# Encoder block on one core: weight scales, neighbourhood bias and gate operands issued in another order

## The chip, the cores and the metric

The kernel runs on one core of a Trainium2 chip. The core has five engines, each of which works through its own queue of instructions in order: PE (TensorE, the matmuls), DVE (VectorE), ACT (ScalarE), POOL (GpSimd) and SP (SyncE, which here issues nearly all DMAs). They wait for one another by semaphores. The metric is device time in microseconds (us); smaller is better.

## The reference

One encoder block on `x` of 1 x 1024 x 1024 in float32: LayerNorm, one wide projection, two attentions beside each other, gates, an output projection and an MLP.

```python
h = layer_norm(x, ln0_g, ln0_b)
proj = h @ w_in + b_in                       # 1024 x 1024 times 1024 x 4352
qa, ka, va, qb, kb, vb, ga, gb = jnp.split(proj, IN_SPLITS, axis=-1)
...
y_na  = neighbourhood_attention(qa, ka, va, na_rpb) @ w_branch_na    # 8 heads, 16 x 64 grid, 8 x 16 window
y_swa = windowed_gqa_with_sink(qb, kb, vb, swa_sink) @ w_branch_swa  # 8 query heads, 2 key heads
mixed = jax.nn.sigmoid(ga) * y_na + jax.nn.sigmoid(gb) * y_swa
h = layer_norm(DEEPNORM_ALPHA * h + mixed @ w_out + b_out, ln1_g, ln1_b)
u = jnp.square(jax.nn.relu(h @ w_ff1 + b_ff1))
h = layer_norm(DEEPNORM_ALPHA * h + u @ w_ff2 + b_ff2, ln2_g, ln2_b)
```

In the neighbourhood attention each head adds a learned bias, `na_rpb`, to its scores before the softmax.

## The kernel before

**Arithmetic.** Every large product is made of 16-bit matmuls. A 32-bit operand is scaled by a power of two and split into a 16-bit `hi` and the 16-bit rest `lo`; `gemm3` and `gemm3_steps` (L399) add hi x hi, hi x lo and lo x hi. The normalised input `h` lies transposed in `hT[:, 0]` (hi) and `hT[:, 1]` (lo), in two halves of 512 tokens. What was 32 bits before the split, the tile `t` of `ln0_turn`, is overwritten later.

**Weight chunks.** `Chunk` holds 1024 x 128 columns of `w_in`, loaded by one DMA of 512 KB. Its method `to(n)` takes it through four states: 1, the squares are summed (ACT, L209); 2, the sum over the partitions (PE, a small f32 matmul, L194), the scale from it (DVE, L196) and its power of two (POOL, `pow`, L198); 3, `hi` (ACT, L236); 4, `lo` (DVE, L238). In attention, `blocks` runs 24 such chunks as fillers, 48 matmuls each. `ahead` puts the states of the next chunk off by so many filler matmuls: `D_C` = 4, 12, 18 for states 2, 3, 4, and 36 for state 1 of the chunk behind it (`D_C0` for the first).

**Stages**, by the times of the profiled execution. Up to 52 us (first stage): `x` comes in, LayerNorm, 64 transposes for each half of the tokens, `ln0_turn` (ACT makes `t`, L368; ACT or DVE makes `hi`; DVE or POOL makes `lo`), and between them the gates of the first two chunks `ws[0]` and `ws[1]`, four times 24 matmuls. A loop over `i` places all this; `LAG` and `LAG2` say how many `i` a gate lies behind the transposes that it reads, `HI_AT` at which `i` the `hi` of `ws[1]` is made, `PRE_AT` at which `i` the third chunk gets its states, and `warm(n)` issues `n` matmuls on zeros. From 52 to 97 us: projections. From 97 to 411 us: attention, one call of `steps(s)` for a quarter of a head: the scores of s + 2 (`part_a`, PE L729 and L730, DVE L731), the exponentials (`part_l`, `part_e`, ACT L750 and L753), the values of s - 1 (`part_c`, PE L837, then ACT L843 and DVE L846 take the result out of PSUM), and filler matmuls between these by `pump`. From 411 to 494 us: the gates' last columns (gate sums). They are computed by a scheme of Strassen's kind with seven products (`STEPS`) for each of four column pairs `p`; its operands are sums of quarters of `h` (A11, A12, A21, A22), formed on DVE by `f_add` (L1135) from the `hi` and `lo` of the quarters (`part`), and sums of quarters of the weights `graw` (`g_sums` L1064, `g_hi` L1080, `g_lo` L1084); `g_do` issues the matmuls (L1095), and `g_after` adds the results up (L1158). From 494 us on: branches, output projection and MLP.

**Order.** PE, ACT, DVE, POOL and SP are scheduled by hand (`manual_schedule`): each engine runs its instructions in the order in which the program issues them, and an instruction that waits holds up all behind it on its engine. `defer` puts a step behind a number of filler matmuls, `flush` issues those that are due.

**Two helpers of attention.** `na_bias(h)` loads a table `tb` and issues eight POOL operations at once: one scaling (L537) and seven adds that make the bias tile `bm` (L541). `proj_na_qk` allocates for the first two heads the tile `kl` and clears half of it on POOL at once (L505).

**Weights of the gate sums.** `g_load(p)` loads the pair `p` in iteration H = 12 + p of the loop over heads; `g_squares` sums its squares on ACT (L209) in H = 13 + p, `g_total` makes its scale after that.

Of the kernel before, what the change touches and what calls it, by code (L numbers as in the profile page):

```python
# [92 lines left out]
def encoder_block(ctx, tc, x, w_in, w_br, w_out, w_ff1, w_ff2, par, rows, rpbp,  # L93
# [96 lines left out]
    def scale_of(ps, sums_, exp=True):  # L190
        j = n_sc[0]
        n_sc[0] += 1
        for i, c in enumerate(sums_):
            PE.matmul(ps[:, 0:2], one0, c.to_broadcast([P, 2]), start=(i == 0), stop=(i == len(sums_) - 1))  # L194
# [1 line left out]
        DVE.scalar_tensor_tensor(out=t, in0=ps[:, 0:2], scalar=Q_MIN, in1=cv0, op0=ALU.max, op1=ALU.mult)  # L196
        if exp:
            POOL.tensor_tensor(out=wsc[:, 2 * j:2 * j + 2], in0=t, in1=pw0, op=ALU.pow)  # L198
# [7 lines left out]
    def square_sum(raw):  # L206
        i = n_sq[0] % 40
        n_sq[0] += 1
        ACT.activation(junk0, raw.rearrange("p k n -> p (k n)"), AF.Square, accum_out=wsq[:, i:i + 1], saturate=False)  # L209
# [11 lines left out]
    class Chunk:  # L221
# [6 lines left out]
        def to(self, n, ps=None, exp=True):  # L228
            while self.n < n:
# [3 lines left out]
                elif self.n == 2:  # L233
                    self.sc, self.back = scale_of(psum("t") if ps is None else ps, [self.sq], exp)
                elif self.n == 3:
                    ACT.activation(self.pair[:, 0], self.raw, AF.Copy, bias=0.0, scale=self.sc)  # L236
# [263 lines left out]
    def proj_na_qk(h, w, store):  # L500
        q = ap.tile([P, S], F32R, tag="q", name="q", bufs=3)
        kk = ap.tile([P, S], F32R, tag="kh", name="kh")
        if h < 2:
# [1 line left out]
            POOL.memset(b32(na_ql[h][64:P]), 0.0)  # L505
# [27 lines left out]

    def na_bias(h):
        tb = ap.tile([P, 16, 3, 8], F32, tag="x2", name="tb", bufs=1)
        nc.sync.dma_start(tb.rearrange("p a g c -> p (a g c)"), rpbp[h])
        POOL.tensor_scalar(out=tb, in0=tb, scalar1=8.0, scalar2=None, op0=ALU.mult)  # L537
        bm = ap.tile([P, 896], F32, tag="x1", name="bm")
        for o, g0, n, m in ((0, 0, 3, mk[:, 0:384]), (384, 1, 2, mk[:, 384:640]), (640, 0, 2, mk[:, 384:640])):
            for g in range(n):  # L540
                POOL.tensor_tensor(  # L541
                    out=bm[:, o + g * P:o + (g + 1) * P].rearrange("p (a c) -> p a c", c=8),
                    in0=tb[:, :, g0 + g, :],
                    in1=m[:, g * P:(g + 1) * P].rearrange("p (a c) -> p a c", c=8), op=ALU.add)
# [1842 lines left out]
```

## Time and profile before

| | us |
|---|---|
| time, median of 3 runs | 1276.07 |
| the runs | 1273.51 to 1277.71 |
| the profiled execution, its own time | 1273.13 |
| its span, first to last instruction | 1271.3 |
| PE busy | 1226.5 (96%) |
| DVE busy | 958.2 (75%) |
| ACT busy | 849.7 (67%) |
| POOL busy | 338.2 (27%) |

The page cuts the span into 40 slices of 31.8 us and gives the busy share of each in tenths; `PEclk` is the clock that the throttle granted to PE, in tenths of full speed, and `DMA` the mean busy share of the 16 DMA engines. For shorter stretches the trace is asked by windows (busy time, count and granted clock in a stretch), by waits (who waited for whom), by groups of equal instructions and by time (one row for an instruction, or for several alike, with its start, its length and, in brackets, the idle time before it and what ended that).

### The profile page before, as it was taken

To read this page: it belongs to the slowest core of one execution; us is meant where nothing else is said; L and a number is where in the kernel's file an instruction comes from. 1 tells how busy PE (TensorE), PEld (TensorE's weight loads), DVE (VectorE), ACT (ScalarE), POOL (GpSimd) and SP (SyncE) were. 2 spreads that over 40 slices of the span, in tenths; PEclk is the share of its full clock that TensorE was granted. 3 is DMA by queue.
4 is the path that set the end of the run, shared out by engine and by line. 5 is a ranking of instruction groups with operands and counts; after the bars stand their busy time and mean duration, and the time that the engine had idled before them with its cause. 6 is when DMAs were issued, how large, how long until landed. Compare 5 with 4: busy or idle time off the path is not lost.

```text
span 1271.3 us, 16827 instructions
## 1 busy us (share of the span) xinstructions
PE 1226.5 (96%) x6026; PEld 672.3 (53%) x6026; DVE 958.2 (75%) x1360; ACT 849.7 (67%) x1368; POOL 338.2 (27%) x353
## 2 busy tenths in 40 slices
PE   7999998899889989999999999999999999999997
PEld 4446555455445436888885444444444444444443
DVE  6678996677657986444687987787776678898888
ACT  6568887888888546442557877877877746435457
POOL 5362222242230000334741013233300001211207
PEclk8999999899999999999999999999999999999999
DMA  5345666457757224656342257676637635363333
GB/s 236 134 181 114 156 148 152 116 129 141 165 147 193 61 91 150 198 192 221 116 167 94 107 179 258 239 247 201 226 140 265 231 132 224 124 245 136 124 108 133
DMA packets 165780, 210.53 MB, mean 166 GB/s; under 512 B 110400, under 2 KB 112192, under 8 KB 159424
## 3 DMA queue, kind: packets, MB, share of 16 engines
q1 hardware_dynamic: 164720, 208.59, 51.8%
q8 instruction: 47, 0.77, 0.2%
q10 hardware_dynamic: 976, 0.87, 0.2%
q14 instruction: 37, 0.30, 0.1%
HBM read 127.55 MB, written 56.18 MB: 145 GB/s over the span
## 4 chain that ended last, share of the span: by engine, by line
PE 72%; ACT 10%; DVE 9%; DMA 4%; issue 2%; POOL 1%; SPq 1%; ACTq 0%; POOLq 0%; DVEq 0%
PE ps_mm L399 12%; PE ps_o L1620 6%; PE ps_t L1620 6%; PE ps_s L2092 6%; PE ps_mm L2092 6%; PE ps_mm L1620 5%; PE ps_t L2092 5%; PE ps_o L2092 4%; DMA pt<-pl 3%; PE ps_s L1620 2%; ACT ss L750 2%; PE ps_o L837 1%; ACT pl L753 1%; PE ps_t L390 1%; PE ps_t L389 1%
## 5 line engine op out<-in xcount | busy, mean ns | idle before, releaser
L399 PE MATMUL ps_mm<-hT 128*128 128x512 f16 x1248 | 298.1, 382 | 5.5 <-DVE hT L196 2.2
L1620 PEld LDWEIGHTS <-tw 128*128 128x128 f16 x1248 | 122.1, 99 | 145.0 <-issue 1.7
L399 PEld LDWEIGHTS <-hT 128*128 128x128 f16 x1248 | 117.8, 100 | 131.2 <-issue 17.3
L2092 PEld LDWEIGHTS <-hS 128*128 128x128 f16 x1008 | 98.6, 98 | 118.3
L750 ACT ACTIVATE ss<-ss,sk 128x384 f32<-128x384 f32 (+1 forms) x128 | 74.1, 580 | 28.5 <-DVE sk L731 27.9
L1620 PE MATMUL ps_t<-hS,tw 128*128 128x512 f16 x384 | 87.9, 379 | 0.0
L762 DVE SCALAR_TENSOR_TENSOR pl<-ss,pl 128x640 f16<-128x640 f32 (+1 forms) x64 | 72.1, 1127 | 1.3 <-ACT pl L753 0.9
L1810 DVE TENSOR_TENSOR usl<-usl 128x512 f32<-128x512 f32 x64 | 51.5, 804 | 23.5 <-ACT usl L1738 23.3
L1375 POOL TENSOR_TENSOR mx<-sg 128x512 f32<-128x512 f32 x16 | 32.5, 2032 | 133.6 <-DMA sg<-sg_d 82.7
L1541 POOL TENSOR_TENSOR c<-c 128x2 f32<-128x2 f32 x16 | 15.5, 974 | 193.5 <-DVE c L1540 193.5
L2112 POOL TENSOR_TENSOR acc<-acc,rst 128x512 f32<-128x512 f32 x16 | 31.3, 1958 | 123.0 <-DMA rst<-xr_d 100.7
L753 ACT ACTIVATE pl<-ss 128x640 f16<-128x640 f32 (+1 forms) x64 | 50.6, 790 | 11.6 <-DMA pt<-pl 9.8
L837 PE MATMUL ps_o<-pt,vv 128*128 128x256 f16 (+1 forms) x448 | 49.7, 251 | 8.5 <-DVE oT L846 8.1
L1095 PEld LDWEIGHTS <-hT 128*128 128x128 f16 x336 | 32.9, 99 | 46.5 <-DVE hT L1084 5.3
L238 DVE SCALAR_TENSOR_TENSOR hT<-hT 128x1024 f16<-128x1024 f32 x26 | 35.4, 1362 | 28.0 <-ACT hT L236 27.9
L1925 DVE SCALAR_TENSOR_TENSOR hS<-stg,c,hS 128x2048 f16<-128x2048 f32 x21 | 49.9, 2378 | 7.6 <-ACT hS L1922 7.6
L1547 DVE SCALAR_TENSOR_TENSOR tw<-raw,c,tw 128x512 f16<-128x512 f32 x60 | 51.8, 864 | 4.7 <-ACT tw L1544 4.3
L198 POOL TENSOR_TENSOR hT<-hT 128x2 f32<-128x2 f32 x29 | 23.6, 816 | 116.7 <-DVE hT L196 116.6
L2092 PEld LDWEIGHTS <-hA 128*128 128x128 f16 x336 | 32.9, 98 | 39.6
L837 PEld LDWEIGHTS <-vv 128*128 128x128 f16 x448 | 35.7, 98 | 26.2 <-DVE oT L846 10.1
L1620 PE MATMUL ps_o<-hS,tw 128*128 128x512 f16 x192 | 44.0, 379 | 0.0
L1544 ACT ACTIVATE tw<-raw,c 128x512 f16<-128x512 f32 x60 | 41.7, 708 | 2.8 <-DVE raw L1585 2.8
(395 smaller groups left out, 3006.3 us busy)
## 6 DMA issues: line engine op xcount, KB each, us to landing
us_d<-usl SPq DMA_DIRECT2D x112, 256.0 KB, 2.9
stg<-us_d SPq DMA_DIRECT2D x28, 1024.0 KB, 4.8
hT<-in_w_in SPq DMA_DIRECT2D x26, 512.0 KB, 4.5
raw<-in_w_ff SPq DMA_DIRECT2D x24, 512.0 KB, 5.5
sg<-sg_d SPq DMA_DIRECT2D x32, 256.0 KB, 3.4
hA<-in_w_ff SPq DMA_DIRECT2D x8, 1024.0 KB, 8.0
hS<-in_w_ff SPq DMA_DIRECT2D x8, 1024.0 KB, 7.6
sg_d<-hT SPq DMA_DIRECT2D x16, 256.0 KB, 3.1
```

Source lines behind the costliest of these rows:

```text
L238: DVE.scalar_tensor_tensor(out=self.pair[:, 1], in0=self.raw, scalar=self.sc, in1=self.pair[:, 0], op0=ALU.mult, op1=ALU.subtract)
L399: PE.matmul(ps, a[:, k, :], act(b, k), start=(k == 0 and i == 0), stop=(k == NK - 1 and i == 2))
L750: ACT.activation(p, p, AF.Exp, bias=nm[:, i:i + 1], scale=-1.0, accum_out=sums_l[o_chunk][:, hh, 2 * t + i:2 * t + i + 1])
L753: ACT.activation(pl[:, 0:n_all], e[:, 0:n_all], AF.Copy, bias=0.0, scale=P_SCALE)
L762: DVE.scalar_tensor_tensor(out=pl[:, n:2 * n], in0=e[:, 0:n], scalar=P_SCALE, in1=pl[:, 0:n], op0=ALU.mult, op1=ALU.subtract)
L837: PE.matmul(o, vs, move(part), start=(m == 0 and part == 0), stop=(m == len(runs) - 1 and part == 1))
L1544: ACT.activation(hi_lo(slot, 0), src, AF.Copy, bias=0.0, scale=w_scale(p))
L1547: DVE.scalar_tensor_tensor(out=hi_lo(slot, 1), in0=src, scalar=w_scale(p), in1=hi_lo(slot, 0), op0=ALU.mult, op1=ALU.subtract)
L1620: PE.matmul(ps, ww, act[:, part, k, :], start=(first and k == 0 and m == 0), stop=(k == 3 and m == 2), skip_group_check=True)
L1810: DVE.tensor_tensor(out=out, in0=a, in1=b, op=op)
L1925: DVE.scalar_tensor_tensor(out=slot[:, :, 1, :], in0=src, scalar=scale, in1=slot[:, :, 0, :], op0=ALU.mult, op1=ALU.subtract)
L2092: PE.matmul(ps, st[:, a, part, j * P:(j + 1) * P], w[:, a, wpart, :], start=(first and a == 0 and m == 0), stop=(a == 3 and m == 2), skip_ ...
```

## The change

Nothing that is computed changes, up to rounding in the quarter sums. Five things are ordered or made in another way:

1. `Chunk.to` has five states: the sum over the partitions (state 2, PE) is apart from the scale (state 3, DVE and `pow` on POOL); `hi` is state 4, `lo` state 5. In attention, within a block of 48 filler matmuls the next chunk's sum and scale come after 2 (4 before), its `hi` after 18 (12 before), its `lo` after 28 (18 before), and the squares of the chunk behind it after 32 (36 before).
2. First stage: the squares and the sum of `ws[1]` move into the first loop over `g`, its `hi` from i = 4 to i = 1, and the gate of `ws[1]` for the first half of the tokens follows that of `ws[0]` after one `i` (three before). `warm` at that place issues two matmuls in place of four.
3. The eight POOL operations of `na_bias` go into a list, from which each call of `steps` takes three; the clearing of `kl` moves behind the projection that fills the tile.
4. The squares of the gate sums' weights are made on DVE in place of ACT, and loads, squares and scales of these weights come one head earlier.
5. `ln0_turn` stores the 32-bit `t` of the quarters A11, A12 and A22 to DRAM (`hq_d`, 12 DMAs of 256 KB, issued by SP); the gate sums load them (3 DMAs of 1 MB, into `gq`, `gq2`, and `gq` again), so that three operand sums take one DVE operation each in place of two. The order of the calls in the gate sums changes with it.

```diff
-LAG2 = 3
+LAG2 = 1
-HI_AT = 4
-PRE_AT = {9: 1, 12: 2, 16: 3, 18: 4}
-D_C = 4, 12, 18, 36
-D_C0 = 16, 26, 32, 38
+HI_AT = 1
+PRE_AT = {9: 1, 12: 3, 16: 4, 18: 5}
+D_C = 2, 18, 28, 32
+D_C0 = 12, 22, 32, 40
-WARM = 18, 4, 4, 2, 0, 4
+WARM = 18, 4, 4, 2, 0, 2
+    hq_d = {q: dp.tile([P, 4, 512], F32, name=f"hq_d{q}") for q in ("A11", "A12", "A22")}
...
-    def scale_of(ps, sums_, exp=True):
+    def total_of(ps, sums_):
+        for i, c in enumerate(sums_):
+            PE.matmul(ps[:, 0:2], one0, c.to_broadcast([P, 2]), start=(i == 0), stop=(i == len(sums_) - 1))
+
+    def scale_of(ps):
...
+        if on_dve:
+            DVE.scalar_tensor_tensor(out=junk0, in0=flat, scalar=1.0, in1=flat, op0=ALU.mult, op1=ALU.mult,
+                                     accum_out=wsq[:, i:i + 1], saturate=False)
...
                 elif self.n == 2:
-                    self.sc, self.back = scale_of(psum("t") if ps is None else ps, [self.sq], exp)
+                    self.ps = psum("t") if ps is None else ps
+                    total_of(self.ps, [self.sq])
                 elif self.n == 3:
+                    self.sc, self.back = scale_of(self.ps)
+                elif self.n == 4:
...
+        q = f"A{half + 1}{k // 4 + 1}"
+        if q in hq_d:
+            nc.sync.dma_start(hq_d[q][:, k % 4], t)
...
-            POOL.memset(b32(na_ql[h][64:P]), 0.0)
...
             def lo(cs=cs, b=b):
+                if h < 2 and cs.start == 0:
+                    POOL.memset(b32(ql[64:P]), 0.0)
...
+        bias_ops.append(lambda: POOL.tensor_scalar(out=tb, in0=tb, scalar1=8.0, scalar2=None, op0=ALU.mult))
...
-                POOL.tensor_tensor(
+                bias_ops.append(lambda o=o, g0=g0, m=m, g=g: POOL.tensor_tensor(
...
+            if g == 3:
+                ws[0].to(3)
             ln0_stats(g)
             if g == 3:
-                ws[0].to(2, start_ps[:, 2:4], False)
+                ws[1].to(2, start_ps[:, 4:6])
...
+            if g == 2:
+                ws[0].to(2, start_ps[:, 2:4])
+                ws[1].to(1)
...
-            if i == 1:
-                ws[1].to(1)
-            if i == 3:
-                ws[1].to(2, start_ps[:, 4:6])
+            if i == 0:
+                ws[1].to(3)
...
             if before_b:
                 before_b()
+            for op in bias_ops[:3]:
+                bias_ops.pop(0)()
             flush(False, True)
...
-            gsq[p, c] = square_sum(graw[p][c])
+            gsq[p, c] = square_sum(graw[p][c], True)
...
+        gq2 = x0p.tile([P, 4, 512], F32, tag="m", name="gq2")
+        nc.sync.dma_start(gq, hq_d["A11"])
+        nc.sync.dma_start(gq2, hq_d["A12"])
...
-        f_add(g2, g1, part("A11", 0), ALU.subtract)
-        f_add(g2, g2, part("A11", 1), ALU.subtract)
+        f_add(g2, g1, gq, ALU.subtract)
+        nc.sync.dma_start(gq, hq_d["A22"])
-        f_add(g1, part("A12", 0), g2, ALU.subtract)
-        f_add(g1, g1, part("A12", 1))
+        f_add(g1, gq2, g2, ALU.subtract)
-        f_add(g2, part("A22", 0), g2, ALU.subtract)
-        f_add(g2, g2, part("A22", 1))
+        f_add(g2, gq, g2, ALU.subtract)
```

What this does to the queues is shown at three places, each with the rows of one engine in the order of the program (line, operation, tile written and tiles read, shape).

POOL in attention, where the first neighbourhood heads begin (at 211 to 220 us of the profile). The rows that write `hT` 128x2 are the `pow` of a weight chunk. Before:

```order
L198 TENSOR_TENSOR hT<-hT 128x2
L537 TENSOR_SCALAR tb<-tb 128x384
L541 TENSOR_TENSOR bm<-tb,mk 128x128 x7
L505 MEMSET kl 64x1024
L198 TENSOR_TENSOR hT<-hT 128x2
```

and of the changed kernel:

```order
L200 TENSOR_TENSOR hT<-hT 128x2
L534 MEMSET kl 64x1024
L551 TENSOR_SCALAR tb<-tb 128x384
L554 TENSOR_TENSOR bm<-tb,mk 128x128 x2
L200 TENSOR_TENSOR hT<-hT 128x2
L554 TENSOR_TENSOR bm<-tb,mk 128x128 x5
```

The second `pow` stood behind eight bias operations and the clearing of `kl`; now it stands behind three bias operations.

ACT in the first stage: `ln<-ln,mv` is the normalisation, L209 the squares, L236 a chunk's `hi`, L367 and L368 the evacuations of `ln0_turn`. Before:

```order
L341 ACTIVATE ln<-ln,mv 128x1024
L236 ACTIVATE hT<-hT 128x1024
L368 ACTIVATE t<-ps_t,hT 128x512
L368 ACTIVATE t<-ps_s,hT 128x512
L209 ACTIVATE hT<-hT 128x1024
L367 ACTIVATE hT<-ps_o,hT 128x512
```

and of the changed kernel, where these lines are 348, 243, 375, 213 and 374:

```order
L348 ACTIVATE ln<-ln,mv 128x1024
L213 ACTIVATE hT<-hT 128x1024
L243 ACTIVATE hT<-hT 128x1024
L375 ACTIVATE t<-ps_t,hT 128x512
L375 ACTIVATE t<-ps_s,hT 128x512
L243 ACTIVATE hT<-hT 128x1024
L374 ACTIVATE hT<-ps_o,hT 128x512
```

The squares of `ws[1]` moved ahead of the `hi` of `ws[0]`, and the `hi` of `ws[1]`, which stood seven instructions behind those squares, took their place.

DVE in the gate sums: the rows with 128x2048 are `f_add` (`g` and `gt` hold 32-bit sums, `gS` is the 16-bit `lo`). Before:

```order
L1135 TENSOR_TENSOR gS_4156<-g_3917,gS_4156 128x2048
L1084 SCALAR_TENSOR_TENSOR hT<-gT_4215,hT 128x512
L1135 TENSOR_TENSOR g_3917<-hT,gt 128x2048
L1084 SCALAR_TENSOR_TENSOR hT<-graw,hT 128x512
L1135 TENSOR_TENSOR g_3917<-g_3917,hT 128x2048
L1084 SCALAR_TENSOR_TENSOR hT<-graw,hT 128x512
L1158 SCALAR_TENSOR_TENSOR go<-ps_s,hT,go 128x512 x2
L1135 TENSOR_TENSOR gt<-hT,gt 128x2048
L1135 TENSOR_TENSOR gS_4158<-g_3917,gS_4158 128x2048
```

and of the changed kernel:

```order
L1154 TENSOR_TENSOR gS_4173<-g_3941,gS_4173 128x2048
L1180 SCALAR_TENSOR_TENSOR go<-ps_s,hT,go 128x512
L1104 SCALAR_TENSOR_TENSOR hT<-graw,hT 128x512
L1154 TENSOR_TENSOR g_3941<-gq_4177,gt 128x2048
L1104 SCALAR_TENSOR_TENSOR hT<-graw,hT 128x512
L1180 SCALAR_TENSOR_TENSOR go<-ps_s,hT,go 128x512
L1154 TENSOR_TENSOR gt<-gt 128x2048
L1154 TENSOR_TENSOR gS_4175<-g_3941,gS_4175 128x2048
```

Between the `lo` of one operand (first row) and that of the next (last row) stood three long sums; now there are two, and both read a loaded quarter where `hi` and `lo` were read before.

More of the change, by code (lines that the diff above doesn't have):

```diff
@@ L188, in encoder_block, with square_sum @@
     n_sc = [0]
-    def scale_of(ps, sums_, exp=True):
+    def total_of(ps, sums_):
+        for i, c in enumerate(sums_):
+            PE.matmul(ps[:, 0:2], one0, c.to_broadcast([P, 2]), start=(i == 0), stop=(i == len(sums_) - 1))
+    def scale_of(ps):
         j = n_sc[0]
         n_sc[0] += 1
-        for i, c in enumerate(sums_):
-            PE.matmul(ps[:, 0:2], one0, c.to_broadcast([P, 2]), start=(i == 0), stop=(i == len(sums_) - 1))
         t = wt[:, 2 * j:2 * j + 2]
         DVE.scalar_tensor_tensor(out=t, in0=ps[:, 0:2], scalar=Q_MIN, in1=cv0, op0=ALU.max, op1=ALU.mult)
-        if exp:
-            POOL.tensor_tensor(out=wsc[:, 2 * j:2 * j + 2], in0=t, in1=pw0, op=ALU.pow)
+        POOL.tensor_tensor(out=wsc[:, 2 * j:2 * j + 2], in0=t, in1=pw0, op=ALU.pow)
         return wsc[:, 2 * j:2 * j + 1], wsc[:, 2 * j + 1:2 * j + 2]
-    def scale_exp(c):
-        POOL.tensor_tensor(out=wsc[:, 0:2], in0=wt[:, 0:2], in1=pw0, op=ALU.pow)
     n_sq = [0]
-    def square_sum(raw):
+    def square_sum(raw, on_dve=False):
         i = n_sq[0] % 40
         n_sq[0] += 1
-        ACT.activation(junk0, raw.rearrange("p k n -> p (k n)"), AF.Square, accum_out=wsq[:, i:i + 1], saturate=False)
+        flat = raw.rearrange("p k n -> p (k n)")
+        if on_dve:
+            DVE.scalar_tensor_tensor(out=junk0, in0=flat, scalar=1.0, in1=flat, op0=ALU.mult, op1=ALU.mult,
+                                     accum_out=wsq[:, i:i + 1], saturate=False)
+        else:
+            ACT.activation(junk0, flat, AF.Square, accum_out=wsq[:, i:i + 1], saturate=False)
         return wsq[:, i:i + 1]
@@ L532, in encoder_block @@
     rt = ap.tile([P, 2, S], F32, tag="vv", name="rt")
+    bias_ops = []
     def na_bias(h):
@@ L1032, in g_squares @@
         def g_squares(p, c):
-            gsq[p, c] = square_sum(graw[p][c])
+            gsq[p, c] = square_sum(graw[p][c], True)
         def g_total(p):
-            gsc[p] = scale_of(psum("t"), [gsq[p, c] for c in range(2)])
+            ps = psum("t")
+            total_of(ps, [gsq[p, c] for c in range(2)])
+            gsc[p] = scale_of(ps)
         for H in range(16):
@@ L1103, in g_prep @@
             g_lo(p, i)
-        assert all(c.n == 4 for c in chunks)
+        assert all(c.n == 5 for c in chunks)
         g_prep(0, 1)
         g_prep(0, 2)
-        for c in range(2):
-            g_squares(3, c)
         steps(62, TAIL)
+        g_prep(1, 1)
         steps(63, TAIL, lambda: g_mm(0, 1))
-        g_prep(1, 1)
-        g_total(3)
+        g_prep(1, 2)
+        g_prep(2, 1)
         steps(64, TAIL, None, lambda: g_mm(0, 2))
+        g_prep(2, 2)
         pump(1000)
@@ L1224, in encoder_block @@
         g_hi(2, 5)
-        f_add(g1, part("A12", 0), g2, ALU.subtract)
+        form_lo("S1", g1)
         g_do(2, 2)
+        g_after(2, 2)
         g_lo(2, 5)
         g_hi(3, 5)
-        f_add(g1, g1, part("A12", 1))
+        f_add(g1, gq2, g2, ALU.subtract)
         g_do(3, 1)
+        form_hi("S4", g1)
         g_lo(3, 5)
         g_hi(2, 3)
-        form_hi("S4", g1)
-        g_after(2, 2)
         g_do(3, 2)
         g_after(3, 2)
+        f_add(g2, gq, g2, ALU.subtract)
         g_hi(3, 3)
-        f_add(g2, part("A22", 0), g2, ALU.subtract)
+        for ks in (slice(0, 2), slice(2, 4)):
+            ACT.copy(gop["S3"][:, 0, ks], g2[:, ks])
         g_do(2, 6)
@@ L1241, in encoder_block @@
         g_lo(2, 3)
-        f_add(g2, g2, part("A22", 1))
+        g_sums(2, 7)
         g_do(3, 6)
         g_lo(3, 3)
-        g_do(2, 5)
-        g_do(3, 5)
-        for ks in (slice(0, 2), slice(2, 4)):
-            ACT.copy(gop["S3"][:, 0, ks], g2[:, ks])
-        g_sums(2, 7)
         g_sums(3, 7)
         g_hi(2, 7)
+        g_do(2, 5)
         for ks in (slice(0, 2), slice(2, 4)):
             f_add(gop["S3"][:, 1, ks], g2[:, ks], gop["S3"][:, 0, ks], ALU.subtract)
+        g_do(3, 5)
         g_lo(2, 7)
```

61 lines of the change are left out of this document (27 added, 34 removed).

## The prediction

> **What bounds the kernel now.** The page comes first: the line of busy times, then the shares of the chain of work that ended last.
>
> ```profile
> PE 1226.5 (96%) x6026; PEld 672.3 (53%) x6026; DVE 958.2 (75%) x1360; ACT 849.7 (67%) x1368; POOL 338.2 (27%) x353
> PE 72%; ACT 10%; DVE 9%; DMA 4%; issue 2%; POOL 1%; SPq 1%; ACTq 0%; POOLq 0%; DVEq 0%
> ```
>
> PE bounds the kernel: it is idle for 1271.3 - 1226.5 = 44.8 us. The change takes two matmuls on zeros from PE and otherwise only moves its work, so it can win idle time, or time in which PE ran at a reduced clock. The view by windows (length, then busy time and count of PE, weight load, DVE, ACT and POOL, granted clock, DMA share, GB/s) shows where these are.
>
> ```profile
> 16.00:18.00 2.00, 0.00 (x0) 0.00 (x0) 1.54 (x2) 2.00 (x4) 0.00 (x0) 0.70 1.05 438
> 18.00:24.00 6.00, 2.96 (x9) 1.52 (x10) 5.79 (x15) 4.16 (x8) 3.50 (x5) 0.50 0.41 164
> 22.00:33.00 11.00, 11.00 (x46) 5.82 (x45) 7.94 (x17) 9.68 (x12) 10.21 (x18) 0.77 0.01 2
> 97.00:219.00 122.00, 118.85 (x705) 71.59 (x704) 106.08 (x211) 103.70 (x220) 33.31 (x49) 1.00 0.66 149
> 219.00:227.00 8.00, 0.70 (x4) 0.20 (x3) 5.39 (x10) 6.29 (x11) 0.69 (x1) 0.66 0.10 22
> 227.00:232.00 5.00, 5.00 (x18) 2.79 (x17) 2.18 (x6) 4.76 (x12) 0.00 (x0) 0.52 0.66 143
> 320.00:411.00 91.00, 83.26 (x472) 47.31 (x472) 59.47 (x120) 77.38 (x152) 21.50 (x31) 1.00 0.71 174
> 411.00:450.00 39.00, 36.02 (x183) 17.14 (x183) 37.18 (x36) 22.05 (x31) 3.80 (x2) 1.00 0.22 60
> 450.00:462.00 12.00, 11.19 (x45) 4.50 (x43) 11.62 (x16) 5.61 (x7) 0.00 (x0) 0.86 0.11 44
> 494.00:1271.30 777.30, 766.21 (x3565) 418.36 (x3562) 583.49 (x687) 480.05 (x685) 201.81 (x170) 1.00 0.51 181
> ```
>
> The reader is to see one hole: PE did 0.70 us of work in the 8 us from 219, and ran at 0.52 of its clock for 5 us after it. The later half of attention loses 91 - 83.26 = 7.7 us. In the gate sums DVE is busy all the time (37.18 of 39 us, 11.62 of 12). The last row, 61% of the time, the change doesn't touch. The view of waits names what PE waited for from 97 to 411 us (total, times, longest).
>
> ```profile
> PE ps_o L837 <- DVE oT L846: 8.1, 3, 7.3
> PE ps_t L194 <- ACT hT L209: 5.3, 6, 1.1
> ```
>
> **A, the hole at 219 us.** The trace in order of time shows what stood behind what.
>
> ```profile
> 211.83 1.55 POOL L537 TENSOR_SCALAR tb<-tb 128x384 f32<-128x384 f32 x1 [18.56 <-DMA tb<-in_rpbp]
> 212.25 0.15 DVE L196 SCALAR_TENSOR_TENSOR hT<-ps_t,hT 128x2 f32<-128x2 f32 x1
> 213.46 3.55 POOL L541 TENSOR_TENSOR bm<-tb,mk 128x128 f32<-128x128 f32 x7
> 217.94 0.95 POOL L505 MEMSET kl<- 64x1024 f32 x1 [0.93 <-PE ps_t L730]
> 218.97 0.72 POOL L198 TENSOR_TENSOR hT<-hT 128x2 f32<-128x2 f32 x1
> 219.72 1.15 ACT L236 ACTIVATE hT<-hT 128x1024 f16<-128x1024 f32 x1 [4.57 <-POOL hT L198]
> 224.93 1.28 DVE L238 SCALAR_TENSOR_TENSOR hT<-hT 128x1024 f16<-128x1024 f32 x1
> 226.12 0.68 DVE L846 TENSOR_TENSOR oT<-ps_o,oT 64x512 f32<-64x512 f32 x1
> 226.86 1.25 PE L837 MATMUL ps_o<-pt,vv 128*128 128x256 f16 x6 [7.30 <-DVE oT L846]
> ```
>
> The weight sum was on DVE at 212.25, but the `pow` of L198 waited on POOL behind the bias of one head (1.55 + 3.55 us), and then behind a MEMSET that itself waited for the attention matmuls. ACT stood still 4.57 us ahead of the `hi` (L236), and DVE's evacuation of the attention result, for which PE waits, came after ACT's copies that stand behind it. Afterwards the `pow` stands behind the scaling and two adds alone: 211.83 + 1.55 + 2 x 0.51 + 0.72 = 215.1 instead of 219.7, which is the whole of ACT's 4.57 us. The `hi` also stands behind more exponentials, and the `lo` (1.28 us) behind the evacuation instead of ahead of it. So the evacuation may end at 226.8 - 4.57 - 1.28, and 0.7 us of waiting is kept for what I can't place: 6.6 us go. With so short a gap I let the reduced clock go too: 5.00 us at 0.52 are 2.4 us lost. Together **-9.0**; bounds 0 (the stall stays) and -9.7 (all of it). What is late next is ACT, 104 of 122 us busy ahead of the hole.
>
> **B, the rest of attention.** PE's 5.3 us for the squares (L209) come from sums issued too soon behind them: 48 - 36 + 4 = 16 matmuls before, 48 - 32 + 2 = 18 now. The eight squares of the gate weights leave ACT for DVE.
>
> ```profile
> L209 ACT ACTIVATE hT<-graw 128x1024 fp8e5<-128x1024 f32 x8 | 8.4, 1051 | 0.1
> L238 DVE SCALAR_TENSOR_TENSOR hT<-hT 128x1024 f16<-128x1024 f32 x26 | 35.4, 1362 | 28.0 <-ACT hT L236 27.9
> ```
>
> ACT, 77.38 of 91 us busy in the later half, loses 8.4 us. DVE gains eight operations that before doesn't show; the nearest row is L238, an operation of the same kind and size, so 8 x 1.362 = 10.9 us, on an engine with 59.47 of 91 us busy. There they are covered while they don't stand ahead of a score or an evacuation. The wait of DVE for `hi` (27.9 us over 26 times) shrinks with the ten matmuls now between `hi` and `lo` (six before). The `bias_ops` in threes cost POOL the same time as at once; POOL has 21.5 of 91 us in use. I take **-3.0**, a good half of the 5.3; bounds -7.7 (all idle time of that half) and +10.9 (every square on DVE in the way).
>
> **C, the gate sums.** DVE is the engine that PE waits for.
>
> ```profile
> 422.84 2.28 DVE L1135 TENSOR_TENSOR gt<-gt,hT 128x2048 f32<-128x2048 f32 x1
> 441.33 5.56 PE L1095 MATMUL ps_t<-gS,hT 128*128 128x512 f16 x25
> 448.55 0.38 PE L1095 MATMUL ps_t<-gS,hT 128*128 128x512 f16 x1 [1.66 <-DVE gS L1135]
> 449.22 6.61 PE L1095 MATMUL ps_t<-gS,hT 128*128 128x512 f16 x22 [0.29 <-DVE hT L1084]
> 461.95 4.26 PE L1095 MATMUL ps_o<-hT 128*128 128x512 f16 x19 [0.81 <-DVE go L1158]
> ```
>
> Three sums of 2.28 us go, 6.8 us of DVE. The waits of 1.66, 0.29 and 0.81 us then end, 2.8 us; and 22 matmuls took 6.61 us at the clock of 0.86 where 25 took 5.56 at full clock, so that at that rate (0.222 us each) they take 4.9: 1.7 us. **-4.5**; at most -6.8, DVE's saving. The other end is a late quarter, of which there are three loads of 1 MB. The first is read where before had the second part of the same sum (422.84), by the new order on DVE some three small operations later, near 425; in SP's order it stands behind the last steps of attention, and I estimate its issue at 418 from these.
>
> ```profile
> stg<-us_d SPq DMA_DIRECT2D x28, 1024.0 KB, 4.8
> hS<-in_w_ff SPq DMA_DIRECT2D x8, 1024.0 KB, 7.6
> sg_d<-hT SPq DMA_DIRECT2D x16, 256.0 KB, 3.1
> ```
>
> From DRAM scratch 1 MB took 4.8 us, from weights 7.6. With the DMA engines 0.22 busy there, 4.8 is the nearer row, and the first load's slack is some 2 us (the others' more); +7.6 is the upper bound.
>
> **D, the first stage.**
>
> ```profile
> 16.34 0.76 ACT L368 ACTIVATE t<-ps_t,hT 128x512 f32<-128x512 f32 x1
> 18.86 0.58 PE L194 MATMUL ps_mm<-hT 128*128 128x2 f32 x2 [3.46 <-ACT hT L209]
> 21.63 1.44 PE L399 MATMUL ps_mm<-hT 128*128 128x512 f16 x3 [2.19 <-DVE hT L196]
> 23.32 0.78 ACT L367 ACTIVATE hT<-ps_s,hT 128x512 f16<-128x512 f32 x1 [1.84 <-PE ps_s L358]
> 23.99 0.77 ACT L368 ACTIVATE t<-ps_s,hT 128x512 f32<-128x512 f32 x1
> 31.74 1.25 ACT L341 ACTIVATE ln<-ln,mv 128x1024 f32<-128x1024 f32 x1
> 51.91 0.78 ACT L652 ACTIVATE hT<-ps_mm,prm,hT 128x512 f32<-128x512 f32 x1 [4.45 <-PE ps_mm L399]
> ```
>
> PE waited 3.46 and 2.19 us for the sum and scale of `ws[1]`; now these lie ahead, and the first gate matmul can start at about 18.5 instead of 21.63. Little of this reaches the end of the stage (51.91): the transposes of the second half wait for the last normalisation, which ACT ends at 33.0. What gains is the work that PE has done by then: two steps of `LAG2` are 6 matmuls of 0.222, 1.3 us; and of ACT's wait of 1.84 us for PE I count 0.7, since the transposes still follow gate matmuls. **-2.0**; at best 1.3 + 1.84 + two zero matmuls of 0.2, -3.5. The 12 stores of `t` (3.1 us by `sg_d`) lie in a stretch with a DMA share of 0.01, but the first meet queues at 1.05. The closest reuse of a single buffer is from the `t` that ended at 17.1 to the one that starts at 23.99, 6.9 us: hidden at 3.1, and +1 as the other bound.
>
> Here the clock bears on the sum. The last matmul ahead of the wait ended at 15.4, and the clock fell within 16 to 18 us (0.70), stayed at 0.50 to 24, and was full only after 26; I leave it so, since this fall came less than 3 us after the last matmul, and the changed gap still has about 3 us. [...]
>
> **Sum.** -9.0 - 3.0 - 4.5 - 2.0 = -18.5. The profiled execution took 1273.13 us by its own time (span 1271.3, and 1.8 around it), which would become 1254.6. That execution is the fast end of the runs; their median is 1276.07, so I predict 1276.07 - 18.5, about **1257.5**.
>
> **The rivals.**
> 1. *The wait moves to DVE.* The squares stand in DVE's queue ahead of scores (L731) and evacuations (L846), PE then waits there, and half of the 10.9 us shows: B is +5.5, the sum -10, 1266. For it speaks that DVE had 106 of 122 us in the earlier half; against it, that the squares fall in the later half, with 65% in use. 0.16.
> 2. *The change doesn't do what it says:* the `pow` is issued sooner, but POOL is held ahead of it by another wait (the 18.56 us for `tb`'s DMA, or the MEMSET, which has moved ahead of the bias and waits for the projection's bank). Then A is 0: -9.5, 1266.6. Against it: `tb` had landed when DVE's sum came. 0.11.
> 3. *The clock stays full in the first stage*, because no gap is long enough any more. Three microseconds at half clock come back, but the second half still waits for ACT, so that at most ACT's wait of 1.84 us is won beyond the 0.7: 1.1 us more, 1256.4. [...] 0.10.
> 4. *Slower:* the stores of `t` hold the single-buffered tiles. ACT then waits at the next `t`, four times, and all transposes behind it. It costs four times what a store takes beyond 6.9 us; to eat 18.5 us and end 0.3% above before, another 3.8, a store must take 6.9 + 22.3 / 4 = 12.5 us, four times the 3.1 of the row. At 13 us the time is 1276.07 - 18.5 + 24.4 = 1282. For it: 438 GB/s are moving at 16 to 18 us; against it: 2 GB/s from 22 to 33. 0.06.
>
> **How the numbers follow.** The forecast has 0.57. About 0.3%, 3.8 us, is what a measurement of this kernel can tell from no change. Faster: the forecast 0.57, rival 3 0.10, of rival 1 0.13, of rival 2 0.08: 0.88. Within 0.3%: 0.03 each of rivals 1 and 2, whose terms can meet, and 0.01 of rival 4: 0.07. Slower: 0.05 of rival 4. The lower end has every term at its best, -9.7 - 7.7 - 6.8 - 3.5 = -27.7: 1248. The upper end takes in rivals 1 and 2 with some 2.5 us above them for a late load: 1269.
>
> **What would show it.** A: the wait of PE on the evacuation of `oT` falls from 7.3 to under 1.5 us, ACT's `hi` waits for no `pow` near 219, and the clock is full from 219 to 240. B: the eight squares on DVE take about 1.36 us each, and 320 to 411 has less than 5 us of idle PE. C: no wait of PE on `gS` over 0.5 us, the clock full at 450 to 462, and no wait of DVE on a load of `gq`. D: the first gate matmul near 18.5, the last gate evacuated near 50, no wait of ACT on a store. The prediction is wrong if PE waits for DVE behind a square, if POOL's `pow` stays late, or if the first stage ends after 51.9.

## The result: slower by 0.6%, and the profile after

The changed kernel takes 1283.6 us (median of 5 runs, 1281.51 to 1285.01), the kernel before beside it 1274.71 us; the ratio is 1.0063, with a 95% interval of 1.0044 to 1.0081. The forecast was 1257.5 us, with a range up to 1269. The profiled execution took 1284.63 us and has a span of 1282.9, 11.6 more than before's.

The page of the changed kernel, with the same two lines as before (busy times, shares of the last chain):

```profile
PE 1230.6 (96%) x6024; PEld 671.9 (52%) x6024; DVE 963.4 (75%) x1373; ACT 841.5 (66%) x1352; POOL 346.0 (27%) x353
PE 71%; DVE 11%; ACT 8%; DMA 5%; issue 3%; POOL 1%; SPq 0%; POOLq 0%; ACTq 0%; DVEq 0%
```

They say little: 4 us more of PE and shares within 2 points. The windows at the places of the forecast say more (columns as in the prediction):

```profile
97.00:219.00 122.00, 112.82 (x641) 65.91 (x639) 100.07 (x198) 97.58 (x207) 26.07 (x37) 0.97 0.61 136
219.00:227.00 8.00, 8.00 (x50) 4.90 (x49) 6.26 (x13) 6.37 (x13) 5.76 (x8) 1.00 0.89 188
320.00:411.00 91.00, 75.66 (x403) 41.78 (x402) 58.51 (x120) 61.66 (x120) 28.78 (x32) 0.94 0.71 152
411.00:450.00 39.00, 37.97 (x207) 19.76 (x206) 33.23 (x45) 24.03 (x40) 2.67 (x1) 1.00 0.55 166
450.00:462.00 12.00, 10.69 (x50) 4.76 (x49) 12.00 (x12) 7.81 (x10) 0.00 (x0) 1.00 0.12 46
```

From 97 to 219 us PE now issues 641 matmuls where it issued 705; from 320 to 411 it is busy for 75.7 us instead of 83.3. Both stretches of attention lost time. The view of waits of PE from 97 to 411 us names new ones:

```profile
PE ps_t L193 <- ACT hT L213: 10.0, 7, 2.2
PE ps_o L850 <- DMA pt<-pl: 5.8, 3, 3.5
PE ps_mm L409 <- ACT hT L665: 3.6, 1, 3.6
PE ps_mm L409 <- ACT vf L469: 2.6, 2, 2.4
```

The wait for the squares (L209 before, L213 now) has nearly doubled from 5.3 us, and a wait for the DMA transposes of the probabilities (`pt<-pl`) has come up.

Windows at fixed times drift apart when one kernel is late. So I also took the same matmul (same line, same number on that line) from both traces and subtracted its start times. Each number is how late, in us, a kernel is against before at that matmul; the head names the place by its time in before. The experiments stand in the same table, all by their one profiled execution:

| | ahead of attention, 92.7 | 205.5 | behind the hole, 234.9 | attention over, 397.9 | gate sums, 464.8 | span |
|---|---|---|---|---|---|---|
| changed kernel | -2.1 | +9.1 | +1.4 | +14.2 | +10.2 | +11.6 |
| e1, old `D_C` | -1.6 | -0.5 | -4.0 | +5.0 | +1.0 | +3.4 |
| e2, old gate weights | -2.1 | +7.0 | -0.2 | +2.1 | -1.6 | -1.8 |
| e3, both old | -1.6 | -0.5 | -5.6 | -0.9 | -4.5 | -4.5 |
| e4, bias alone | -0.1 | +0.9 | -3.8 | -1.5 | -1.5 | -1.1 |
| e5, e3 with `lo` late | -1.9 | -1.7 | -7.6 | -4.8 | -8.4 | -7.7 |
| e6, e3 with `hi` late, `lo` soon behind | +3.1 | +21.8 | +18.8 | +26.2 | +22.6 | +22.9 |
| e7, e3 with squares on DVE | -1.7 | -0.8 | -5.6 | +0.5 | -2.0 | -1.8 |
| e8, e3 with earlier loads | -1.8 | -1.1 | -5.9 | -0.6 | -4.6 | -4.6 |
| e9, e5 with `hi` late | -1.7 | +9.1 | +1.9 | +6.8 | +3.2 | +3.0 |
| e10, gate sums alone | -0.2 | +0.6 | -0.1 | +2.0 | -1.6 | -1.8 |
| e11, e5 with split loads | -1.5 | -0.9 | -6.8 | -11.5 | -15.1 | -14.2 |
| e12, e3 without the first stage | +0.1 | +0.2 | -6.2 | -1.0 | -4.6 | -4.6 |

Small differences in this table are not readings. The executions shown of e1 and e3 are the slowest of their 12 and 6 runs, that of e2 is the fastest of its 12. And e10, which changes nothing between 52 and 400 us, still drifts by 0.8 us between 92.7 and 205.5 and by 2.1 us between 234.9 and 397.9.

The first row tells where it went. First stage -2.1, hole -7.7, gate sums -4.0: three terms of the forecast are there. Attention around them lost 11.2 us by 205 us and 12.8 more between 235 and 398, of which some 2 may be the drift that e10 shows too. Of the 11.2 us, 5.2 are longer waits for the squares (7.1 us from 97 to 219 us, 1.9 before) and up to 3.4, by estimate, the two stretches of 3.41 us at a clock of 0.50 that follow two of these waits (last section). The last 1.4 us came behind 465 us, most of it where the change touches nothing.

### The profile page after: what moved, and what is told of

Its sections match the earlier page's. It is cut to its first block, busy times and chain, and to the rows that moved or that the text cites. A ratio compares the mean times of both kernels' runs of the same rounds, so it can differ in the third digit from the quotient of the medians.

```text
span 1282.9 us, 16853 instructions
## 1 busy us (share of the span) xinstructions
PE 1230.6 (96%) x6024; PEld 671.9 (52%) x6024; DVE 963.4 (75%) x1373; ACT 841.5 (66%) x1352; POOL 346.0 (27%) x353
## 4 chain that ended last, share of the span: by engine, by line
PE 71%; DVE 11%; ACT 8%; DMA 5%; issue 3%; POOL 1%; SPq 0%; POOLq 0%; ACTq 0%; DVEq 0%
PE ps_mm L409 12%; PE ps_o L1636 6%; PE ps_t L1636 6%; PE ps_mm L2108 6%; PE ps_s L2108 6%; PE ps_mm L1636 5%; PE ps_t L2108 5%; PE ps_o L2108 4%; DMA pt<-pl 4%; PE ps_s L1636 2%; PE ps_o L850 1%; ACT pl L766 1%; PE ps_o L401 1%; PE ps_t L401 1%; PE ps_t L400 1%
## 5 line engine op out<-in xcount | busy, mean ns | idle before, releaser
L409 PE MATMUL ps_mm<-hT 128*128 128x512 f16 x1248 | 302.5, 386 | 10.8 <-ACT hT L665 3.6
L766 ACT ACTIVATE pl<-ss 128x640 f16<-128x640 f32 (+1 forms) x64 | 50.6, 790 | 36.3 <-DMA pt<-pl 34.6
L1115 PEld LDWEIGHTS <-hT 128*128 128x128 f16 x336 | 32.6, 98 | 43.3 <-DVE hT L1104 2.2
L245 DVE SCALAR_TENSOR_TENSOR hT<-hT 128x1024 f16<-128x1024 f32 x26 | 35.8, 1378 | 17.6 <-ACT hT L243 17.5
```

Of the source, the lines that this page charges most:

```text
L245: DVE.scalar_tensor_tensor(out=self.pair[:, 1], in0=self.raw, scalar=self.sc, in1=self.pair[:, 0], op0=ALU.mult, op1=ALU.subtract)
L409: PE.matmul(ps, a[:, k, :], act(b, k), start=(k == 0 and i == 0), stop=(k == NK - 1 and i == 2))
L766: ACT.activation(pl[:, 0:n_all], e[:, 0:n_all], AF.Copy, bias=0.0, scale=P_SCALE)
```

## The experiments

The kernel before was measured again beside each group of experiments, and its median lay between 1274.71 and 1276.27 us, so the ratios to it are the ones to compare. A difference of ratios is given in us of its 1275.

**e1, e2, e3: which part costs the time.** The old numbers of the chunk schedule (e1), the old gate weights (e2), both (e3):

```diff
-D_C = 2, 18, 28, 32
-D_C0 = 12, 22, 32, 40
+D_C = 4, 12, 18, 36
+D_C0 = 16, 26, 32, 38
```

```diff
-            gsq[p, c] = square_sum(graw[p][c], True)
+            gsq[p, c] = square_sum(graw[p][c])
...
-                if 11 <= H < 15 and i == 1:
-                    g_load(H - 11)
+                if H >= 12 and i == 1:
+                    g_load(H - 12)
```

> The changed kernel with the old numbers D_C = 4, 12, 18, 36 and D_C0 = 16, 26, 32, 38; all else as changed. Theory 1 (the later hi and lo in attention make the squares behind them on ACT late, and PE waits for the sums): the three waits of 2.2 us at 110, 163 and 199 us and the two stretches of half clock behind them go, the delay against before at 205 us falls from +9.1 to about +1, and the time is about 8 us below the changed kernel (ratio to before about 1.000). Theory 2 (the earlier weight loads and the squares on DVE cost the time, in the last heads): the waits up to 220 us may change, the stalls at 324, 376 and 403 us stay; at most 3 us below the changed kernel. Theory 3 (attention is bound by ACT and DVE there, so that the lead of the first stage is lost whatever the numbers are): the waits of PE move elsewhere, and the delay at 205 us stays above +6.

> The changed kernel with the gate sums' weights as before: loads one head later, squares on ACT, scales later. Theory 2: the stalls of PE at 324 us (2.1), 376 us (3.6) and 403 us (3.6) and the half clock behind them go, and the time is about 10 us below the changed kernel (ratio to before about 0.999). Theory 1 and theory 3: the stalls of the first heads (up to +9 us at 205 us) stay; of the last heads' delay at most 4 us go.

> Both undone: the old D_C and D_C0, and the gate sums' weights as before. If theories 1 and 2 together explain the loss, the first stage's -2, the hole's -9 and the gate sums' -4 are left: about 1260 us, ratio to before 0.988. Theory 3: the time stays within 5 us of before, since the lead is lost to ACT and DVE in attention.

Measured: e1 1273.24 us, ratio 0.9989 [0.9979, 0.9998]; e2 1273.71 us, 0.9996 [0.9986, 1.0005]; e3 1266.04 us, 0.9934 [0.9921, 0.9946]. Against the changed kernel's 1.0063 each undoing takes off some 0.7% (9 us), and the second on top of the first still 0.55 to 0.62%. In the table e1 has the loss up to 205 us gone (+9.1 to -0.5) and keeps a loss between 235 and 398 (9.0 us), e2 the other way round. Theories 1 and 2 both hold, each for its place. Theory 3, that the lead of the first stage is lost anyway, holds for 1.1 us at most: e1 and e3 come to 92.7 with -1.6 and to 205.5 with -0.5. That is hardly more than the 0.8 to 1.0 us by which e10 and e4, which have no lead, drift there. e3 stays 6 us above the 1260 that I expected if the two theories explained everything: its hole gives 5.1 us, not 9, and between 235 and 398 it loses 4.7 us again, of which the drift of e10 is 2.1. The execution shown is also 2.6 us above e3's median; the rest stays open.

**e5, e6, e9: which of the chunk's numbers.** On e3, first `lo` alone late (e5, with D_C0 = 16, 26, 40, 38, by which in the first block alone `hi` is made at 38 too, right ahead of `lo`; e5 comes to 92.7 us with -1.9, e3 with -1.6):

```diff
-D_C = 4, 12, 18, 36
+D_C = 4, 12, 28, 36
```

then `hi` late with `lo` soon behind it (e6, with D_C0 = 16, 32, 36, 38):

```diff
-D_C = 4, 12, 18, 36
+D_C = 4, 18, 22, 36
```

then one number on e5 (e9, with its D_C0):

```diff
-D_C = 4, 12, 28, 36
+D_C = 4, 18, 28, 36
```

> As the run with both undone (old D_C, D_C0 and gate weights), but lo alone late: D_C = 4, 12, 28, 36 and D_C0 = 16, 26, 40, 38, which on DVE is the place of the changed kernel, while hi stays at its old place on ACT. Theory 1a (the later hi, closer ahead of the squares on ACT, makes the sums late): the waits for the squares stay at 0.5 to 1 us, the delay at 205 us stays near -0.5, and the rest of the hole at 222 us (3.3 us) shrinks to under 1 us: about 1263 us. Theory 1b (the later lo, which stands ahead of the score operations on DVE, makes the squares late): the three waits of 2.2 us at 110, 163 and 199 us are back, about 1274 us.

> As the run with both undone, but hi late and lo soon behind it: D_C = 4, 18, 22, 36 and D_C0 = 16, 32, 36, 38. Theory 1a: the waits of 2.2 us are back, the delay at 205 us is +5 or more, about 1274 us. Theory 1b: they stay away, about 1266 us.

> As the run with lo alone late, with one number changed: hi at 18 in place of 12 (D_C = 4, 18, 28, 36; D_C0 unchanged), which puts hi and lo on ACT and DVE where the changed kernel has them. Theory 1a (lo then waits on DVE for hi, ahead of the scores, so that exponentials and squares come late and PE waits for the sum): the waits of about 2.2 us for the squares at 160 and 195 us are back, the delay at 205 us rises from about -1.7 to +5 or more, the rest of the hole at 220 us shrinks, and the time is 1271 to 1275 us. If only the two other numbers (sum at 2, squares at 32) cost the time: it stays at 1265.

Measured: e5 1264.53 us, ratio 0.9915 [0.9893, 0.9937]; e6 1295.44 us, 1.0157 [1.0138, 1.0177]; e9 1274.47 us, 0.9990 [0.9978, 1.0002]. The one number, `hi` after 18 matmuls in place of 12, costs 0.75%, 9.5 us; the late `lo` alone costs nothing. The two other numbers cost nothing that can be told: e2 has the sum at 2 and the squares at 32, e9 has them at 4 and 36 (the first block differs too), and they come to 0.9996 and 0.9990. The view of waits of PE from 97 to 219 us has for the squares in e5

```profile
PE ps_t L193 <- ACT hT L213: 2.8, 3, 1.5
```

and in e9, where the changed kernel has 7.1 us,

```profile
PE ps_t L193 <- ACT hT L213: 7.8, 4, 2.2
```

The mechanism is seen by putting the same quarter of a head side by side. In the changed kernel:

```profile
156.92 1.13 ACT L243 ACTIVATE hT<-hT 128x1024 f16<-128x1024 f32 x1
158.09 1.28 DVE L245 SCALAR_TENSOR_TENSOR hT<-hT 128x1024 f16<-128x1024 f32 x1 [1.44 <-ACT hT L243]
159.29 0.61 DVE L744 CUSTOM_DVE_ANT_0 ss<-ps_s,bd,snk 128x384 f32<-128x384 f32 x1
162.20 1.04 ACT L213 ACTIVATE hT<-hT 128x1024 fp8e5<-128x1024 f32 x1
163.39 0.38 PE L193 MATMUL ps_t<-hT 128*128 128x2 f32 x2 [2.20 <-ACT hT L213]
```

and in e5:

```profile
147.41 1.13 ACT L243 ACTIVATE hT<-hT 128x1024 f16<-128x1024 f32 x1
151.80 1.28 DVE L245 SCALAR_TENSOR_TENSOR hT<-hT 128x1024 f16<-128x1024 f32 x1
153.00 0.61 DVE L744 CUSTOM_DVE_ANT_0 ss<-ps_s,bd,snk 128x384 f32<-128x384 f32 x1
155.92 1.04 ACT L213 ACTIVATE hT<-hT 128x1024 fp8e5<-128x1024 f32 x1
157.10 0.38 PE L193 MATMUL ps_t<-hT 128*128 128x2 f32 x2 [1.15 <-ACT hT L213]
```

Where `hi` (L243) comes late, `lo` (L245) waits on DVE for it, 1.44 us, and behind `lo` in DVE's queue stands the score operation (L744). That makes the exponentials on ACT late, the squares (L213) behind them, and PE's sum. With `hi` a quarter of a head earlier, `lo` finds its input ready: 5.3 us from `lo` to the sum in both, but no wait ahead of it. So both parts of theory 1 are in it: `hi` is late on ACT, and `lo` is the operation that passes the delay on. (In this quarter ACT had also waited 1.32 us for a transpose just ahead of `hi`; what the place of `hi` costs by itself is e9's number.)

DVE's wait ahead of `lo` from 97 to 219 us (total, times, longest) is in the changed kernel

```profile
DVE hT L245 <- ACT hT L243: 10.2, 6, 2.4
```

in e9

```profile
DVE hT L245 <- ACT hT L243: 10.6, 7, 2.4
```

and in e6

```profile
DVE hT L245 <- ACT hT L243: 16.0, 6, 4.1
```

Before, e3 and e5 have none over 0.1 us in this stretch. Summed over the whole kernel the same wait doesn't tell a fast version from a slow one: it is 25.5 us in e3, 1.9 in e5 and 18.2 in e9, because e3, like before, has it in the later heads. What follows the times is ACT's wait for the scores from 97 to 219 us: 8.4 us before, 7.0 in e3 and 8.1 in e5, but 12.7 in the changed kernel, 13.5 in e9 and 20.8 in e6. That `hi` is the number that costs is shown by e9; that `lo` passes the delay on is read from these rows, since no run has a late `hi` with `lo` out of the way.

e6, with only four matmuls between the two, is the worst, and 21 us above what either theory said. DVE's wait ahead of `lo` is 46.0 us there over the whole kernel, and PE stood still for DVE's evacuation at several heads as it did at 219 us before (14.9 us in six waits from 97 to 425 us). Part of its loss is another: it comes to 92.7 us 4.7 us later than e3, by a loss in the first block near 62 us, whose `hi` it also put later.

**e7, e8: which part of the gate weights.** On e3, the squares on DVE alone, and the earlier loads, squares and scales alone with the squares on ACT:

> As the run with both undone, but the squares of the gate weights on DVE (loads still one head later). Theory 2a (the squares on DVE stand ahead of scores and evacuations): the stalls of the last heads are back, 4 to 8 us above the run with both undone. Theory 2b (it is the earlier loads: attention's transposes queue behind them in the DMA rings): within 2 us of the run with both undone.

> As the run with both undone, but loads, squares and scales of the gate weights one head earlier, squares on ACT. Theory 2b: the transposes behind the loads land after 8 to 9 us instead of 3 to 4, PE stalls near 318 us and 390 us, and the time is 5 to 8 us above the run with both undone. Theory 2a: within 2 us of it.

Measured: e7 1271.29 us, ratio 0.9971 [0.9955, 0.9988]; e8 1268.46 us, 0.9946 [0.9927, 0.9965]; e3 has 0.9934. The squares on DVE cost 0.37%, 4.7 us; the earlier loads 0.12%, 1.5 us, which the intervals don't set apart from nothing, though the stalls of PE at 317 and 391 us are there (2.2 us each). Theory 2a is shown, 2b at most in part. But e8 only compares two places for the loads; that they cost time at the old place too is seen in e11. The changed kernel's squares are these:

```profile
L210 DVE SCALAR_TENSOR_TENSOR hT<-graw 128x1024 fp8e5<-128x1024 f32 x8 | 10.4, 1298 | 0.1
```

10.4 us on an engine with a third of its time free, of which some 4.7 reached PE. In the order of the changed kernel seven of the eight stand directly ahead of a score operation (L744), and ACT's wait for the scores from 97 to 411 us is 32.6 us in e7, 26.5 in e3. What the loads do when they go wrong is seen on SP's queue. The loads of the same head (H = 14) stand there before as follows (start, time from the first issue to the end of the last, operation), and the view of the tile `pt` says when these two transposes landed:

```profile
382.63 0.89 SPq L1030 DMA_DIRECT2D graw<-in_w_in  x2
385.59 3.32 SPq L765 DMA_TRANSPOSE pt<-pl  x2
DMA to landing us min/median/max: 3.3/3.6/3.8
```

and in the changed kernel, with the waits of ACT and PE behind them:

```profile
390.89 0.95 SPq L1046 DMA_DIRECT2D graw<-in_w_in  x2
391.95 8.40 SPq L778 DMA_TRANSPOSE pt<-pl  x2
DMA to landing us min/median/max: 8.1/8.6/9.2
401.24 0.74 ACT L766 ACTIVATE pl<-ss 128x640 f16<-128x640 f32 x1 [6.21 <-DMA pt<-pl]
402.83 1.44 PE L409 MATMUL ps_mm<-hT 128*128 128x512 f16 x3 [3.63 <-ACT hT L665]
```

Issued 3 us behind 1 MB of loads, two transposes landed after 3.3 and 3.8 us; issued at once, after 8.1 and 9.2. ACT's next step of the probabilities (L766, which writes `pl`) waited 6.21 us for the first of them, the evacuation of a gate (L665) stood behind it, and PE waited 3.63 us for its bank. The earlier place didn't create this: before, a transpose issued at once behind the loads of H = 13, at 360 us, landed after 7.5 us.

**e11: does a load ahead of the transposes cost time?** On e5, the two loads of a pair in successive quarters of a head:

```diff
-                if H >= 12 and i == 1:
-                    g_load(H - 12)
+                if H >= 12 and 1 <= i <= 2:
+                    g_load(H - 12, i - 1)
```

> As the run with lo alone late, but the two loads of a gate weight pair issued in two successive quarters of a head instead of back to back (0.5 MB each ahead of attention's transposes instead of 1 MB). If the stalls at 334, 359 and 386 us come from transposes that queue behind the loads, transposes land sooner (under 6 us each there) and 2 to 4 us are won: about 1261 us. If not: within 1 us of 1264.5.

Measured: 1258.75 us, ratio 0.9864 [0.9851, 0.9878], 0.5% below e5: more than expected, in the place expected (e11 falls from -6.8 to -11.5 between 235 and 398 us, where e5 loses 2.8). The reason is only half as foreseen. The transposes at these places still took 4.7 to 8.8 us to land, 6.4 to 9.4 in e5. But the stalls of PE at 334 and 386 us shrank from 2.3 to 0.7 and from 2.7 us to nothing, and the one stretch of half clock there, 3.4 us, is gone (mean clock 0.98 from 320 to 411 us in e5, 1.00 from 312 to 403 us in e11). That splitting the loads wins is shown; by which of these steps is not. This is the best version: 17.5 us faster than before measured beside it.

**e4, e10, e12: the parts of the forecast by themselves.** The kernel before with the bias portions alone, with the gate sums alone, and with both (e3 without the first stage):

> The kernel before with the bias in portions and the clearing of kl moved, nothing else. The prediction's term A: the hole of 7.3 us at 219 us goes, with its half clock: about -9 us, ratio 0.993. Rival: the portions slow POOL and DVE beside each other (the adds took 792 ns in the changed kernel, 618 before), and half of it comes back in later heads: -4 us, ratio 0.997.

> The kernel before with the stored quarters and the new order of the gate sums, nothing else. Term C of the prediction, -4.5: about 1270.5 us, ratio 0.9965; PE gains 3 to 4 us between 410 and 470 us and nothing elsewhere, and the 12 stores cost nothing up to 52 us. Rival: DVE's sums were hidden, or the stores slow the first stage: within 1 us of before.

> The kernel before with the bias in portions and the gate sums as changed: the run with both undone without its first stage. Term D says that the first stage is worth 2 us: about 1268 us. If attention, bound by ACT and DVE at its sums, eats that lead: within 0.7 us of the run with both undone (1266).

Measured: e4 1271.14 us, ratio 0.9978 [0.9968, 0.9988]; e10 1271.96 us, 0.9968 [0.9955, 0.9980]; e12 1268.66 us, 0.9941 [0.9927, 0.9954]. The gate sums alone win 4.1 us, as forecast. The bias portions alone win 2.8 us, a third of term A and less than either expectation: they are worth 4.7 us at the hole, where 3.3 us of waiting stay, in e4 as in e3. In e4:

```profile
223.76 0.72 PE L840 MATMUL ps_o<-pt,vv 128*128 128x256 f16 x6 [3.33 <-DVE oT L849]
```

in e3:

```profile
222.33 1.25 PE L850 MATMUL ps_o<-pt,vv 128*128 128x256 f16 x6 [3.33 <-DVE oT L859]
```

The late `lo` of e5 takes this to 2.14 us, the late `hi` of the changed kernel to 0.63. Whether the first stage is worth anything at the end can't be told from e12: 0.9941 against 0.9934 lie within each other's intervals. In the traces the two differ by 1.6 us at 92.7, by 0.7 at 205.5, and by 0.1 in the span.

## Why the prediction was wrong, step by step

**A, -9.0: right in kind, 7.7 in size.** The `pow` came before the rest of the bias, as the order said, and the evacuation was only 0.63 us late:

```profile
222.56 1.48 POOL L554 TENSOR_TENSOR bm<-tb,mk 128x128 f32<-128x128 f32 x2
224.00 0.71 POOL L200 TENSOR_TENSOR hT<-hT 128x2 f32<-128x2 f32 x1
229.27 0.72 PE L850 MATMUL ps_o<-pt,vv 128*128 128x256 f16 x6 [0.63 <-DVE oT L859]
```

The clock stayed at 1.00 from 219 to 232. But 1.3 to 1.8 us of this came with the late `hi` (e5, without it, wins 5.9 us there, e9, with it, 7.2), whose price elsewhere I had put at nothing: A counted the gain of a number at one head, and B did not count the same number at all the other heads.

**B, -3.0: the step that failed.** In the trace it was +24 us (11.2 and 12.8, some 2 of it perhaps drift). The sum took the later `hi` and `lo` of the 24 chunks as free, and the squares on DVE as covered. Three things in it were wrong.

First, "16 matmuls before, 18 now" between squares and sum. `flush` only acts at three points of a quarter of a head, so small steps of `D_C` are rounded away: in the order of the program the first six sums in attention stand behind 340, 388, 436, 484, 532 and 580 filler matmuls in both kernels, and the squares behind the same exponentials. Nothing had moved there that could shorten a wait for the squares.

Second, the wait of DVE for `hi` "shrinks". In total it did, from 28.0 to 17.6 us, but the total hides the place. Before had it in the later heads (24.5 us from 219 to 411 us), and there it fell to 5.7. From 97 to 219 us, where before had next to none, 10.2 us came up, three of the six times directly ahead of a score operation, on the path to PE. e9 prices the later `hi` at 9.5 us. I had named the wait, but not what is queued behind it on DVE.

Third, the squares on DVE, "covered while they don't stand ahead of a score or an evacuation". Some did: 4.7 us by e7, 0.6 us for each, which is close to the half of 10.9 that the first rival gave. That rival was right in mechanism; it had no term for the chunk schedule, and so its 1266 was also too low. A smaller miss: the bias adds in threes did not cost POOL the same. The 56 of them took 0.79 us each in the changed kernel and 0.66 in e4, against 0.62 before; no run shows what that cost PE.

Over both lies a cost that I had left out: the clock. I took a reduced clock to follow only a hole of several microseconds; that was my estimate, and no run shows it. In the changed kernel the clock was at 0.50 for 3.41 us behind two waits of PE of 2.2 us, at 110 and 199 us, which by estimate cost 1.7 us each beyond the wait (the last section).

**C, -4.5: right.** -3.6 us in the trace of e10, -4.1 by its time; 4.0 in the changed kernel. DVE waited for no loaded quarter, and no wait of PE on `gS` is left; the clock is at 1.00 from 409 to 1275 us, where before it was at 0.86 from 450 to 462.

**D, -2.0: right at its place, -2.1 at 92.7 us,** but I had carried it to the end unchanged. 0.2 to 1.1 us of it was gone by 205 us in the versions with the early `hi`, which the drift of e4 and e10 there (1.0 and 0.8) doesn't set apart from nothing, and e12 finds no gain at the end that can be told. The reduced clock of that stage, which I had left as it was, lasted 3.4 us instead of 10 (0.50 from 16.26 to 19.67 us; before, from 16.80 to 27.04), so the third rival came about in part, without a gain that shows at 92.7 us. Which gap is too short for a fall, on which that rival rests, no run shows; here the clock fell behind a wait of PE of 2.23 us that ended at 16.00. No wait of ACT on a store is in the trace up to 52 us, so the fourth rival, the stores, did not come about. The second rival did not either.

The single terms were worked out where the profile showed a wait. What decided was an edit that touched 24 chunks and that I had judged by its largest effect, at one of them.

## What to carry to other kernels

A number that a schedule applies to every block has to be followed through an ordinary block as well as the one with the stall: who waits for the moved instruction, and what stands behind that reader on its engine. Look at the program's order before counting distances, since a coarse flush may round a change away or double it. The two late numbers can be had apart, the reader late and the writer early, and a bulk load split over two steps of the program did more here (6.5 us, 0.5%) than most of the change.
